# One layer of a hybrid encoder in float32: a bank, early loads and a summed mean in the projection, and w2's first groups stored in the first block

## Chip, cores, metric

One core of a Trainium2 chip runs the whole program. The metric is the device time of one execution in microseconds (us); the median of several runs counts.

## The reference

One layer over 2048 tokens of width 1024. A normed input goes through one projection `w_in`; its columns feed three mixers, whose outputs go together through `w_out`; then follows an MLP with squared ReLU, and a last norm. Cut to what matters:

```python
h = _rmsnorm(x, g_attn)
p = h @ w_in                                        # 2816 columns
y_a = a_b * _causal_dwconv(a_c * a_h, w_conv_a)     # mixer A, width 3, 256 channels
g = b_glu[..., :256] * sigmoid(b_glu[..., 256:])
g = _causal_dwconv(g, w_conv_b) + b_conv_b          # mixer B, width 31
y_b = silu(_layernorm(g, ln_b_g, ln_b_b))           # mean and variance over 256 channels
# mixer C: stick-breaking attention, 8 heads of 64, strictly causal
z = q @ k.T / 8; log_beta = log_sigmoid(z); log_1m = where(mask, log_beta - z, 0)
a = where(mask, exp(log_beta + suffix_sums_of(log_1m)), 0); o = a @ v
x = x + concat([y_a, y_b, y_c]) @ w_out
h2 = _rmsnorm(x, g_ffn)
x = x + square(relu(h2 @ w_ff1)) @ w_ff2            # 1024 -> 4096 -> 1024
out = _rmsnorm(x, g_final)
```

## The kernel before

Everything lies with channels on the 128 partitions and tokens along the row. A token block `tb` is 512 tokens; there are four. Every large product is made of three matmuls (`mm3`): each factor is split into a rounded high half and the rest (`split`: a ScalarE copy makes the high half, a VectorE or GpSimd subtraction the low one).

*Projection.* It runs in two halves of two token blocks (`p_start`, `p_half`). Each unit of 256 columns of `w_in` is split in the first half, stored in DRAM (`WS`) and loaded in the second. Around it `weave` runs side generators, each advanced in proportion to the main loop's progress (cost, first and last point): `mixer_b`, in the second half also `attention` for the first queries of each head (i = 0), and `pre_split`, which splits `w_out` and the first four chunks of `w1` and stores them. Mixer B has its 31 taps on VectorE in the one PSUM bank "c"; then a mean over 256 channels by matmul with a constant matrix, the variance, a power on GpSimd (`rsqrt`, L118) and its spread over partitions by matmul (`spread`, L134). PSUM banks here: d 3, c 1, z 2, q 1, o 1.

*Attention.* `a_pass1` makes the scores of a key group (bank z), their sigmoids and running products, and ends with `a_cross_a`, the chain across partitions on VectorE: a transpose into a PSUM tile `X`, a scan and some small products into `T`. `a_pass2` multiplies by the transposed chain (`Q`, bank q), splits and multiplies with the values (bank o). Pass 2 of one head runs beside pass 1 of the next.

*Blocks.* `block(tb)` then does, for each token block, the product with `w_out`, the MLP in 32 chunks of `w1` (`ffn1`) and 8 groups of four chunks with `w2` (`ffn2`), and the end (`finish_`); attention for later queries is woven in. `unit` and `w2_piece` bring the weights in by `piece`: in the first block(s) raw weights are loaded and split, then the halves are stored, and later blocks load the halves. Four buffers hold pieces of `w1`/`w_out`, three those of `w2`, five raw loads and other tiles of tag `xt`. `need1` and `need2` ask for the next ones. In the first block the second half of a `w2` piece gets its low half by an accumulating transfer issued by GpSimd (`split_dma`).

Almost all transfers go through the SP queue, in one order; a transfer that has to wait holds all behind it. The order of instructions on each engine and queue is set before the run by a planner, from the program's order, priorities and its own estimates of durations.

Of the kernel before, what the change touches and what calls it, by code (L numbers as in the profile page):

```python
# [15 lines left out]
P = 128  # L16
# [5 lines left out]
HD = 64  # L22
# [46 lines left out]
class Trunk:  # L69
# [78 lines left out]
    def consts(self, ctx):  # L148
# [5 lines left out]
        t = c.tile([P, DC], F32, name="g_attn")  # L154
        nc.scalar.dma_start(t, a["g_attn"].rearrange("(d p) -> p d", p=P))
        self.gvec["g_attn"] = t
# [23 lines left out]
    def vectors(self):  # L180
        nc, tc, a, c = self.nc, self.tc, self.a, self.c
        for name in ("g_ffn", "g_final"):
            t = c.tile([P, DC], F32, name=name)
            self.dma(t, a[name].rearrange("(d p) -> p d", p=P))
            self.gvec[name] = t
        self.wa = c.tile([P, 2, 3], F32, name="wa")
        self.dma(self.wa, a["w_conv_a"].rearrange("(c p) k -> p c k", p=P))
        self.wb = c.tile([P, 2, 31], F32, name="wb")
        self.dma(self.wb, a["w_conv_b"].rearrange("(c p) k -> p c k", p=P))
        self.vb = {}  # L190
        for name in ("b_conv_b", "ln_b_g", "ln_b_b"):
            t = c.tile([P, 2], F32, name=name)
            self.dma(t, a[name].rearrange("(c p) -> p c", p=P))
            self.vb[name] = t
# [246 lines left out]
    def mixer_b(self, hf):  # L441
        nc = self.nc
        for tb in (2 * hf, 2 * hf + 1):
            acc = []
            for c in range(2):
# [10 lines left out]
                nc.scalar.activation(acc[c], t, AF.Copy)  # L456
            for _ in range(3):
                yield 1.8
            mean = self.psum("ps_mean", "c")
            for c in range(2):  # L460
                nc.tensor.matmul(mean, self.avg, acc[c], start=c == 0, stop=c == 1)
            sqs = []
# [9 lines left out]
            yv = self.rsqrt(self.colsum(sqs[:1], "c"), 1.0 / 256.0, LN_EPS)  # L472
            for _ in range(4):
                yield 1.8
# [71 lines left out]
    def a_pass1(self, g):  # L546
# [36 lines left out]
        A0.append(t)  # L583
        yield 1
        tot = self.a_cross_a(g, Rd, None)
        if not i:
# [23 lines left out]
    def a_cross_a(self, g, R, seed):  # L610


        nc = self.nc
        X = self.ps.tile([P, TB], F32, name="ps_t", tag="z", bufs=self.banks["z"])
        T = self.at.tile([P, TB + 1], F32, name="T", tag="T1" if seed is None else "T2", bufs=1)
        nc.vector.transpose(X, R)
# [18 lines left out]
        nc.vector.tensor_tensor(q3, q3, C.unsqueeze(2).to_broadcast([P, 16, 32]), op=ALU.mult)  # L635
        g["qd" if seed is None else "ql"] = qt
        return tot

    def a_pass2(self, g):
# [37 lines left out]
        for x in late:  # L677
            self.a_av(g, o, n, *x)
        tmp = pool.tile([P, TB], F32, name="otmp", tag="om", bufs=ab["om"])[:HD]
        nc.scalar.activation(tmp, o[HD:P], AF.Copy)  # L680

        if h % 2 == 0:
            self.yc = self.st.tile([P, TB], F32, name="yc", tag="y", bufs=self.ab["yc"])
        nc.vector.tensor_tensor(self.yc[HD * (h % 2) : HD * (h % 2) + HD], o[0:HD], tmp, op=ALU.add)
        if h == H - 1 and i:
# [26 lines left out]
    def attention(self, groups):  # L712
# [3 lines left out]
        for n in range(len(groups) + 1):  # L716
# [5 lines left out]
            d1 = d2 = 0.0  # L722
            live1, live2 = g is not None, prev is not None

            lag = 0 if prev and prev["i"] else 2
            while live1 or live2:
                if live2 and (not live1 or (d2 + lag) * max(n1, 1) <= d1 * max(n2, 1)):
                    try:
# [5 lines left out]
                elif live1:  # L734
                    try:
                        next(p1)
                        d1 += 1
# [90 lines left out]
    def block(self, tb, before):  # L828
# [140 lines left out]
        yield from ffn1(0, 1)  # L969
        need2(1)  # L970

# [4 lines left out]
        yield from ffn1(2)  # L976
        need2(2)
        ms = self.spread(mt, "z")
        for d in range(DC):
            if d == DC // 2:  # L980
                yield from ffn1(3)
            nc.vector.tensor_tensor(acc[d], acc[d], ms, op=ALU.mult)
        ss2 = hp.tile([P, TB], F32, name="ss2", tag="ss", bufs=2)
        sq7 = []
        for c in range(4, FC):
            yield from ffn1(c)
            if c < w2b:
                need2(c)
            if c % G == 0 and not (tb == 3 and c == FC - G):
# [8 lines left out]
        else:  # L998
# [8 lines left out]
            self.finish(tb, acc, [ss2] + sq7, em, right)  # L1007
            for _ in fin:
# [6 lines left out]

    def finish_(self, tb, acc, sums, em, cols=slice(0, TB)):
        nc, a, hp = self.nc, self.a, self.hp
# [4 lines left out]
        yield  # L1022
        R = self.spread(y, "z", bs)
        yield
        for d in range(DC):
            t = acc[d] if tb == 3 else hp.tile([P, TB], F32, name="ot", tag="ot", bufs=self.ob)
            t = t[:, cols]
            nc.vector.scalar_tensor_tensor(t, acc[d][:, cols], self.gvec["g_final"][:, d : d + 1], R[:, cols], op0=ALU.mult, op1=ALU.mult)
            (nc.scalar if tb == 3 and d % 2 else nc.sync).dma_start(a["out"][d * P : (d + 1) * P, ts], t)
            yield  # L1030

    def build(self):
        tc = self.tc
        with ExitStack() as ctx:
# [6 lines left out]
            with ExitStack() as c1:  # L1041
# [12 lines left out]
                self.ab = dict(Kl=1, A0=6, om=2, Alo=2, Ahi=2, Vl=1, late=1, yc=2)  # L1054
                weave(self.p_half(0), [(Side(self.mixer_b(0)), 115, 20, 225, True), (Side(self.x_norms()), 24, 60, 180, True)])
                self.heads = {}
                a0 = Side(self.attention([(h, 0) for h in range(H)]))
                weave(self.p_half(1), [(Side(self.mixer_b(1)), 116, 0, 200, True), (a0, 28, 0, 210, True), (Side(self.pre_split()), len(self.presplit), 0, 200, True)])
            with ExitStack() as c2:
# [67 lines left out]
```

## Time and profile before

| | us |
|---|---|
| three runs | 2421.49, 2425.93, 2416.74 |
| their median | 2421.49 |
| the profiled execution | 2415.74 |
| its span, first to last instruction | 2414.0 |
| TensorE busy in it | 2379.1 |
| VectorE, GpSimd, ScalarE busy | 1534.0, 1128.6, 1043.6 |

The granted clock of TensorE was 0.997 on average. Times in the profile count from the start of the span: the projection lies up to about 545, block 0 to about 1035, blocks 1 and 2 take about 485 us each, and block 3 the rest. A busy TensorE is not one at its peak, since matmuls are pipelined; the count of matmuls in a stretch tells more.

### The profile page before, as it was taken

To read this page: it belongs to the slowest core of one execution; us is meant where nothing else is said; L and a number is where in the kernel's file an instruction comes from. 1 tells how busy PE (TensorE), PEld (TensorE's weight loads), DVE (VectorE), ACT (ScalarE), POOL (GpSimd) and SP (SyncE) were. 2 spreads that over 40 slices of the span, in tenths; PEclk is the share of its full clock that TensorE was granted. 3 is DMA by queue.
4 is the path that set the end of the run, shared out by engine and by line. 5 is a ranking of instruction groups with operands and counts; after the bars stand their busy time and mean duration, and the time that the engine had idled before them with its cause. 6 is when DMAs were issued, how large, how long until landed. Compare 5 with 4: busy or idle time off the path is not lost.

```text
span 2414.0 us, 32476 instructions
## 1 busy us (share of the span) xinstructions
PE 2379.1 (99%) x11316; PEld 2005.3 (83%) x11316; DVE 1534.0 (64%) x2436; ACT 1043.6 (43%) x1906; POOL 1128.6 (47%) x1133
## 2 busy tenths in 40 slices
PE   8999999999999999999999999999999999999998
PEld 7888877898888888878888888888888888888887
DVE  7966698943898887766676768476667625212114
ACT  5232423342666666544555555355555522121121
POOL 0342477640676666425666665268788720000000
PEclk9999999999999999999999999999999999999999
DMA  7569987789788778687777777866677556655555
GB/s 258 200 234 341 299 269 233 223 265 280 209 225 245 229 206 222 186 300 245 253 234 229 220 242 214 289 200 198 187 202 204 175 183 221 224 187 192 201 183 192
DMA packets 237059, 549.04 MB, mean 227 GB/s; under 512 B 26720, under 2 KB 100448, under 8 KB 218464
## 3 DMA queue, kind: packets, MB, share of 16 engines
q1 hardware_dynamic: 180304, 480.89, 58.9%
q0 software_dynamic: 37504, 56.64, 11.0%
q10 hardware_dynamic: 19088, 9.44, 1.4%
q8 instruction: 89, 1.46, 0.2%
q14 instruction: 74, 0.61, 0.1%
HBM read 390.38 MB, written 148.11 MB: 223 GB/s over the span
## 4 chain that ended last, share of the span: by engine, by line
PE 84%; DMA 6%; DVE 6%; issue 1%; ACT 1%; POOL 1%; SPq 1%; POOLq 0%; DVEq 0%; ACTq 0%
PE ps_y L107 9%; PE ps_y L105 9%; PE ps_y L103 9%; PE ps_u L103 9%; PE ps_u L105 9%; PE ps_u L107 9%; PE ps_p L107 4%; PE ps_p L105 4%; PE ps_p L103 3%; PE ps_z L522 2%; PE ps_z L523 2%; PE ps_x L103 2%; PE ps_x L105 2%; PE ps_x L107 2%; PE ps_o L710 2%; PE ps_o L709 2%
## 5 line engine op out<-in xcount | busy, mean ns | idle before, releaser
L90 POOL TENSOR_TENSOR Alo<-A,Ahi 128x512 fp32r<-128x512 f32 x288 | 385.3, 1347 | 147.0 <-ACT Ahi L88 69.9
L958 DVE TENSOR_TENSOR acc<-acc,ps_y 128x512 f32<-128x512 f32 (+1 forms) x264 | 175.7, 667 | 193.5 <-PE ps_y L107 191.4
L103 PE MATMUL ps_u<-hh,w 128*128 128x512 f32 x1024 | 279.4, 392 | 6.4 <-DMA w<-s_w 6.1
L103 PE MATMUL ps_y<-fh,w 128*128 128x512 f32 (+1 forms) x1056 | 281.2, 384 | 0.0
L105 PE MATMUL ps_y<-fh,w 128*128 128x512 f32 (+1 forms) x1056 | 279.7, 383 | 0.1
L602 POOL TENSOR_TENSOR A<-A,R 128x512 f32<-128x512 f32 x168 | 222.4, 1326 | 121.7 <-ACT A L600 103.3
L107 PE MATMUL ps_y<-fl,w 128*128 128x512 f32 (+1 forms) x1056 | 278.6, 383 | 0.1
L105 PE MATMUL ps_u<-hh,w 128*128 128x512 f32 x1024 | 276.1, 390 | 0.3 <-DVE w L90 0.3
L107 PE MATMUL ps_u<-hl,w 128*128 128x512 f32 x1024 | 275.8, 390 | 0.0
L118 POOL TENSOR_TENSOR rs_y<-rs_v,mhalf 128x4 f32<-128x4 f32 (+1 forms) x13 | 13.2, 1017 | 530.9 <-DVE rs_v L117 486.0
L922 ACT ACTIVATE ps_u<-ps_u 128x512 f32<-128x512 f32 x128 | 74.7, 583 | 399.3 <-PE ps_u L107 399.1
L932 DVE TENSOR_TENSOR fl<-ps_u,fh 128x512 fp32r<-128x512 f32 x128 | 87.7, 685 | 223.3 <-ACT fh L931 222.9
L105 PEld LDWEIGHTS ps_y<-fh,w 128*128 128x128 f32 x1056 | 195.0, 188 | 39.8 <-DMA w<-wraw 0.5
L107 PEld LDWEIGHTS ps_y<-fl,w 128*128 128x128 f32 x1056 | 195.0, 188 | 39.4 <-DVE fl L932 0.6
L88 ACT ACTIVATE Ahi<-A 128x512 fp32r<-128x512 f32 x288 | 176.6, 627 | 117.8 <-PE ps_o L709 51.3
L105 PEld LDWEIGHTS ps_u<-hh,w 128*128 128x128 f32 x1024 | 192.1, 188 | 41.5 <-DVE w L90 0.7
L107 PEld LDWEIGHTS ps_u<-hl,w 128*128 128x128 f32 x1024 | 192.1, 188 | 40.1
L103 PEld LDWEIGHTS ps_y<-fh,w 128*128 128x128 f32 x1056 | 193.6, 188 | 36.8
L103 PEld LDWEIGHTS ps_u<-hh,w 128*128 128x128 f32 x1024 | 186.9, 188 | 42.4 <-DMA w<-s_w 8.1
L604 DVE TENSOR_TENSOR R<-ps_z,R 128x512 f32<-128x512 f32 x168 | 115.7, 689 | 150.6 <-ACT ps_z L601 128.3
L452 DVE SCALAR_TENSOR_TENSOR ps_c<-g,wb,ps_c 128x512 f32<-128x512 f32 x240 | 179.9, 749 | 4.9
L90 DVE TENSOR_TENSOR w<-wraw,w 128x512 fp32r<-128x512 f32 x152 | 150.4, 1008 | 23.7 <-ACT w L88 23.2
(171 smaller groups left out, 4750.7 us busy)
## 6 DMA issues: line engine op xcount, KB each, us to landing
w<-s_w SPq DMA_DIRECT2D x200, 512.0 KB, 3.9
w<-s_w SPq DMA_DIRECT2D x68, 1024.0 KB, 4.8
wraw<-in_w SPq DMA_DIRECT2D x192, 256.0 KB, 5.0
w<-s_w_out SPq DMA_DIRECT2D x64, 512.0 KB, 5.0
s_w<-w SPq DMA_DIRECT2D x32, 1024.0 KB, 5.5
s_w<-w SPq DMA_DIRECT2D x56, 512.0 KB, 4.5
Qd<-KQ SPq DMA_DIRECT2D x64, 256.0 KB, 6.3
xraw<-in_xT SPq DMA_DIRECT2D x48, 256.0 KB, 4.5
```

The costliest lines, as they stand in the source:

```text
L88: nc.scalar.activation(hi, x, AF.Copy)
L90: e.tensor_tensor(lo, x, f(hi), op=ALU.subtract)
L103: self.nc.tensor.matmul(ps, wh, xh, start=start and k == 0, stop=False)
L105: self.nc.tensor.matmul(ps, wl, xh, start=False, stop=False)
L107: self.nc.tensor.matmul(ps, wh, xl, start=False, stop=stop and k == n - 1)
L452: nc.vector.scalar_tensor_tensor(t, g[:, k : k + TB], self.wb[:, c, k : k + 1], t, op0=ALU.mult, op1=ALU.add)
L522: nc.tensor.matmul(z[:, oc], keys, g["qh"][:, qc], start=k == 0, stop=False)
L602: nc.gpsimd.tensor_tensor(t, t, R, op=ALU.mult)
L604: nc.vector.tensor_tensor(Rn, z, R, op=ALU.mult)
L922: nc.scalar.activation(ps, ps, AF.Relu)
L932: nc.vector.tensor_tensor(lo, ps, f(hi), op=ALU.subtract)
L958: nc.vector.tensor_tensor(acc[d][:, cols], acc[d][:, cols], ps, op=ALU.add)
```

## The change

- `consts`, `vectors`: the small parameter vectors are laid out on the host as their tiles lie in SBUF, so each partition's numbers are contiguous in DRAM.
- `mixer_b`: the two channel halves are added on GpSimd (`both`), and one matmul instead of two makes the mean; four instead of three steps stand before it, and six instead of four before the spread. The weave's costs and ends go with it: `mixer_b` 130 to 225 in the first half and 130 to 224 in the second (before 115 and 116 to 225 and 200), attention to 212, `pre_split` to 205.
- `attention`, `a_pass1`, `a_cross_a`: for i = 0 the chain's `X` takes bank q instead of one of z, and pass 1 waits, in the program's order, until the previous head's pass 2 is through.
- `a_pass2`: the upper half of the head's output is copied into the result's place and the lower added there, without the tile `otmp`.
- `pre_split`: the raw load of the next piece is asked for before the present one is split.
- `piece`: `w2`'s groups 0 and 1 (eight pieces) are split and stored in block 0 and loaded from block 1 on; groups 2 to 7 stay as they were (split in blocks 0 and 1, stored in block 1). Accumulating transfers are used for groups 2 to 7 alone.
- `block`: from block 1 on, `w2`'s first pieces are asked for later and one at a time.
- the last block's end: the right half's first two rows of tiles are scaled by `g_final` on ScalarE beforehand and multiplied on GpSimd by a copy of the norm, the other six on VectorE as before.

```diff
@@ mixer_b
-            for _ in range(3):
+            both = self.mx.tile([P, TB], F32, name="sum", tag="sq", bufs=2)
+            nc.gpsimd.tensor_tensor(both, acc[0], acc[1], op=ALU.add)
+            for _ in range(4):
                 yield 1.8
             mean = self.psum("ps_mean", "c")
-            for c in range(2):
-                nc.tensor.matmul(mean, self.avg, acc[c], start=c == 0, stop=c == 1)
+            nc.tensor.matmul(mean, self.avg, both, start=True, stop=True)
...
-            for _ in range(4):
+            for _ in range(6):
                 yield 1.8
             R = self.spread(yv, "c")
@@ a_pass1, a_cross_a
+        if not i:
+            while not g["free"]():
+                yield None
         tot = self.a_cross_a(g, Rd, None)
...
-        X = self.ps.tile([P, TB], F32, name="ps_t", tag="z", bufs=self.banks["z"])
+        X = self.psum("ps_t", "z" if g["i"] else "q")
@@ attention
+            if g:
+                g["free"] = lambda: not live2
...
-                if live2 and (not live1 or (d2 + lag) * max(n1, 1) <= d1 * max(n2, 1)):
+                if live2 and (not live1 or d1 > n1 or (d2 + lag) * max(n1, 1) <= d1 * max(n2, 1)):
...
-                        next(p1)
+                        if next(p1) is None:
+                            d1 = n1 + 1e-3
+                            continue
@@ piece
-        first = -1 if (name, *at) in self.presplit else {"w_out": 0, "w1": 0, "w2": 1}[name]
+        first = -1 if (name, *at) in self.presplit else int(name == "w2" and at[0] > 1)
...
-                if name == "w2" and tb == 0 and part is parts[-1][0]:
+                if name == "w2" and tb < first and part is parts[-1][0]:
@@ pre_split
-        for name, c, q in self.presplit:
-            raw = self.w_raw(self.unit_source(name, c, q))
+        nxt = self.w_raw(self.unit_source(*self.presplit[0]))
+        yield 1
+        for n, (name, c, q) in enumerate(self.presplit):
+            raw = nxt
+            if n + 1 < len(self.presplit):
+                nxt = self.w_raw(self.unit_source(*self.presplit[n + 1]))
@@ block
         yield from ffn1(0, 1)
-        need2(1)
+        if not tb:
+            need2(1)
...
         yield from ffn1(2)
-        need2(2)
+        need2(2 if not tb else 0)
...
                 yield from ffn1(3)
+                need2(1)
...
-            if c < w2b:
-                need2(c)
+            if c == G:
+                need2(w2b - 1)
@@ finish_ (right half of the last block)
+            Rs = hp.tile([P, TB], F32, name="Rs", tag="ot", bufs=self.ob)
+            nc.scalar.activation(Rs[:, cols], R[:, cols], AF.Copy)
...
+            if d in scaled:
+                nc.gpsimd.tensor_tensor(t, t, Rs[:, cols], op=ALU.mult)
```

More of the change, by code (lines that the diff above doesn't have):

```diff
@@ L154, in consts @@
         t = c.tile([P, DC], F32, name="g_attn")
-        nc.scalar.dma_start(t, a["g_attn"].rearrange("(d p) -> p d", p=P))
+        nc.scalar.dma_start(t, a["g_attn"])
         self.gvec["g_attn"] = t
@@ L183, in vectors @@
             t = c.tile([P, DC], F32, name=name)
-            self.dma(t, a[name].rearrange("(d p) -> p d", p=P))
+            self.dma(t, a[name])
             self.gvec[name] = t
         self.wa = c.tile([P, 2, 3], F32, name="wa")
-        self.dma(self.wa, a["w_conv_a"].rearrange("(c p) k -> p c k", p=P))
+        self.dma(self.wa, a["w_conv_a"])
         self.wb = c.tile([P, 2, 31], F32, name="wb")
-        self.dma(self.wb, a["w_conv_b"].rearrange("(c p) k -> p c k", p=P))
+        self.dma(self.wb, a["w_conv_b"])
         self.vb = {}
@@ L192, in vectors @@
             t = c.tile([P, 2], F32, name=name)
-            self.dma(t, a[name].rearrange("(c p) -> p c", p=P))
+            self.dma(t, a[name])
             self.vb[name] = t
@@ L678, in a_pass2 @@
             self.a_av(g, o, n, *x)
-        tmp = pool.tile([P, TB], F32, name="otmp", tag="om", bufs=ab["om"])[:HD]
-        nc.scalar.activation(tmp, o[HD:P], AF.Copy)
         if h % 2 == 0:
             self.yc = self.st.tile([P, TB], F32, name="yc", tag="y", bufs=self.ab["yc"])
-        nc.vector.tensor_tensor(self.yc[HD * (h % 2) : HD * (h % 2) + HD], o[0:HD], tmp, op=ALU.add)
+        y = self.yc[HD * (h % 2) : HD * (h % 2) + HD]
+        nc.scalar.activation(y, o[HD:P], AF.Copy)
+        nc.vector.tensor_tensor(y, y, o[0:HD], op=ALU.add)
         if h == H - 1 and i:
@@ L1006, in block @@
                         next(fin, None)
-            self.finish(tb, acc, [ss2] + sq7, em, right)
+            scaled = (0, 1)
+            for d in scaled:
+                nc.scalar.activation(acc[d][:, right], acc[d][:, right], AF.Copy, scale=self.gvec["g_final"][:, d : d + 1])
+            self.finish(tb, acc, [ss2] + sq7, em, right, scaled)
             for _ in fin:
@@ L1014, in finish, with finish_ @@
                 pass
-    def finish_(self, tb, acc, sums, em, cols=slice(0, TB)):
+    def finish_(self, tb, acc, sums, em, cols=slice(0, TB), scaled=()):
         nc, a, hp = self.nc, self.a, self.hp
@@ L1023, in finish_ @@
         R = self.spread(y, "z", bs)
+        if scaled:
+            Rs = hp.tile([P, TB], F32, name="Rs", tag="ot", bufs=self.ob)
+            nc.scalar.activation(Rs[:, cols], R[:, cols], AF.Copy)
         yield
@@ L1027, in finish_ @@
             t = t[:, cols]
-            nc.vector.scalar_tensor_tensor(t, acc[d][:, cols], self.gvec["g_final"][:, d : d + 1], R[:, cols], op0=ALU.mult, op1=ALU.mult)
+            if d in scaled:
+                nc.gpsimd.tensor_tensor(t, t, Rs[:, cols], op=ALU.mult)
+            else:
+                nc.vector.scalar_tensor_tensor(t, acc[d][:, cols], self.gvec["g_final"][:, d : d + 1], R[:, cols], op0=ALU.mult, op1=ALU.mult)
             (nc.scalar if tb == 3 and d % 2 else nc.sync).dma_start(a["out"][d * P : (d + 1) * P, ts], t)
@@ L1054, in build @@
                 self.ab = dict(Kl=1, A0=6, om=2, Alo=2, Ahi=2, Vl=1, late=1, yc=2)
-                weave(self.p_half(0), [(Side(self.mixer_b(0)), 115, 20, 225, True), (Side(self.x_norms()), 24, 60, 180, True)])
+                weave(self.p_half(0), [(Side(self.mixer_b(0)), 130, 20, 225, True), (Side(self.x_norms()), 24, 60, 180, True)])
                 self.heads = {}
                 a0 = Side(self.attention([(h, 0) for h in range(H)]))
-                weave(self.p_half(1), [(Side(self.mixer_b(1)), 116, 0, 200, True), (a0, 28, 0, 210, True), (Side(self.pre_split()), len(self.presplit), 0, 200, True)])
+                weave(self.p_half(1), [(Side(self.mixer_b(1)), 130, 0, 224, True), (a0, 28, 0, 212, True), (Side(self.pre_split()), len(self.presplit) + 1, 0, 205, True)])
             with ExitStack() as c2:
@@ L1108 @@
         ),
-        "g_attn": lay(np.asarray(inputs["g_attn"])[0]),
-        "w_conv_a": lay(np.asarray(inputs["w_conv_a"])[0].T),
-        "w_conv_b": lay(np.asarray(inputs["w_conv_b"])[0].T),
-        "b_conv_b": lay(np.asarray(inputs["b_conv_b"])[0]),
-        "ln_b_g": lay(np.asarray(inputs["ln_b_g"])[0]),
-        "ln_b_b": lay(np.asarray(inputs["ln_b_b"])[0]),
-        "g_ffn": lay(np.asarray(inputs["g_ffn"])[0]),
-        "g_final": lay(np.asarray(inputs["g_final"])),
+        "g_attn": lay(np.asarray(inputs["g_attn"])[0].reshape(DC, P).T),
+        "w_conv_a": lay(np.asarray(inputs["w_conv_a"])[0].reshape(3, 2, P).transpose(2, 1, 0)),
+        "w_conv_b": lay(np.asarray(inputs["w_conv_b"])[0].reshape(31, 2, P).transpose(2, 1, 0)),
+        "b_conv_b": lay(np.asarray(inputs["b_conv_b"])[0].reshape(2, P).T),
+        "ln_b_g": lay(np.asarray(inputs["ln_b_g"])[0].reshape(2, P).T),
+        "ln_b_b": lay(np.asarray(inputs["ln_b_b"])[0].reshape(2, P).T),
+        "g_ffn": lay(np.asarray(inputs["g_ffn"])[0].reshape(DC, P).T),
+        "g_final": lay(np.asarray(inputs["g_final"]).reshape(DC, P).T),
     }
```

## The prediction

> **What bounds the kernel now.** I read the page's busy shares first, then the busy times of a few stretches, then what TensorE waited for in those that lose time, and last the rows around the longest waits.
>
> ```profile
> PE 2379.1 (99%) x11316; PEld 2005.3 (83%) x11316; DVE 1534.0 (64%) x2436; ACT 1043.6 (43%) x1906; POOL 1128.6 (47%) x1133
> ```
>
> TensorE is busy in 2379.1 of 2414.0 us. So a change pays here only if it takes matmuls out or fills some of the 34.9 us in which TensorE stands. Busy times by stretch (us busy of TensorE, weight loads, VectorE, ScalarE and GpSimd, granted clock, DMA share, GB/s) tell where those are:
>
> ```profile
> 300.00:420.00 120.00, 110.14 (x506) 89.62 (x505) 112.02 (x158) 38.06 (x74) 92.12 (x95) 0.97 0.78 256
> 420.00:480.00 60.00, 60.00 (x287) 50.37 (x287) 58.57 (x95) 17.97 (x31) 38.94 (x43) 1.00 0.67 211
> 620.00:740.00 120.00, 118.03 (x555) 97.94 (x555) 107.95 (x171) 76.06 (x143) 85.04 (x87) 1.00 0.76 215
> 1020.00:1140.00 120.00, 114.90 (x526) 95.22 (x525) 75.91 (x122) 50.79 (x92) 42.21 (x43) 1.00 0.77 262
> 2040.00:2100.00 60.00, 58.37 (x264) 48.11 (x263) 20.14 (x32) 12.36 (x21) 0.00 (x0) 1.00 0.67 242
> 2100.00:2160.00 60.00, 60.00 (x267) 49.67 (x266) 10.44 (x16) 10.58 (x18) 0.00 (x0) 1.00 0.56 199
> ```
>
> The last row is the undisturbed rate: 267 matmuls in 60 us, 0.225 us each. The first (projection, second half of the tokens) loses 9.9 us while VectorE is busy in 112.0 of 120; the third (block 0) 2.0; the fourth (start of block 1) 5.1; the fifth (start of block 3) 1.6. TensorE's waits in 240 to 420, at the start of block 1 and at the start of block 3 (total, times, longest):
>
> ```profile
> PE ps_z L522 <- DVE T L635: 3.4, 1, 3.4
> PE ps_z L522 <- ACT A L537: 2.7, 1, 2.7
> PE ps_R L134 <- POOL rs_y L118: 1.7, 1, 1.7
> PE ps_p L103 <- DVE u L355: 1.0, 1, 1.0
> ```
> ```profile
> PE ps_u L103 <- DMA w<-s_w: 4.7, 4, 1.6
> ```
> ```profile
> PE ps_u L103 <- DMA w<-s_w: 1.4, 2, 1.0
> ```
>
> **The change part by part.**
>
> *Mean of a sum.* The chain of waits and the group table give the mean's price, and GpSimd's full-width product that of the new addition:
>
> ```profile
> 226.77 1.72 PE ps_mean L461 x4
> ```
> ```profile
> L461 PE MATMUL ps_mean<-cb,avg 128*128 128x512 f32 x16 | 7.7, 604 | 0.4 <-ACT cb L456 0.4
> ```
> ```profile
> L602 POOL TENSOR_TENSOR A<-A,R 128x512 f32<-128x512 f32 x168 | 222.4, 1326 | 121.7 <-ACT A L600 103.3
> ```
>
> Four token blocks take 4 passes each, 1.72 us. One matmul instead of two halves that: 4 x 0.86 = 3.4 us less on the bounding engine. The sum costs GpSimd 4 x 1.33 us, and GpSimd has 28 us free in 300 to 420. In front of it stand selects and low halves of the same queue; behind it only the mean waits. The one further step (1.8 x 224/130 = 3.1 us of the main loop) covers the 1.33. Ends: -3.4, and +1.9 if each mean waits out its addition (4 x 1.33 - 3.4). I take -3.4, since idle GpSimd time is near.
>
> *The chain's bank.* For the first queries of each head the cross chain sits in one of two score banks from the transpose to the last product:
>
> ```profile
> 317.79 0.72 DVE L616 STREAM_TRANSPOSE ps_t<-R 128x512 f32<-128x512 f32 x1
> ...
> 324.69 0.68 DVE L635 TENSOR_TENSOR T<-T,ps_t 128x512 f32<-128x512 f32 x1
> ```
>
> That holds it for 7.6 us, because convolution taps are queued between the chain's steps, and the next head's scores pay the 3.4 us wait. In bank q only VectorE writes and reads, so no other engine waits for it. The new condition puts the chain behind the previous head's second pass, whose last use of q is a VectorE product: queued behind it are taps and evacuations of the same engine, which TensorE needs. Two more steps (6.2 us) before the spread cover the 1.7 us wait for rs_y. So 5.1 us are addressed. What is late next is VectorE itself: 112.0 us of its work in 300 to 420 cannot end before 412, so no more than 8.0 of the 9.9 can come back, and the evacuation wait (1.0, u) grows. I give 1.1 back and take -4.0. Ends: -8.0 and 0.
>
> *Loads ahead.* The 2.7 us wait for ScalarE starts elsewhere: ScalarE stood before a split, and the SP queue before a store of ya (waits of SP in 240 to 480).
>
> ```profile
> 364.05 1.15 ACT L88 ACTIVATE wph<-wraw 128x512 fp32r<-128x512 f32 x2 [6.52 <-issue]
> ```
> ```profile
> SPq L79 <- DVE ya L365: 21.2, 3, 11.5
> ```
>
> The idle 6.52 us names no raw load; the split's two output buffers have to be stored first, and those stores queue behind ya. A raw load issued one step earlier does not free them. I count 0; the 2.7 stays in the range.
>
> *w2's first two groups, block 0.* Eight pieces: each loses ScalarE's negated copy and GpSimd's accumulating transfer and gains a VectorE subtraction and a 1 MB store. Rows: the subtraction's group and one with nothing beside it, the SP queue's waits in 620 to 740, the transfers' sizes and landings.
>
> ```profile
> L90 DVE TENSOR_TENSOR w<-wraw,w 128x512 fp32r<-128x512 f32 x152 | 150.4, 1008 | 23.7 <-ACT w L88 23.2
> ```
> ```profile
> 654.60 0.68 DVE L90 TENSOR_TENSOR w<-wraw,w 128x512 fp32r<-128x512 f32 x1
> ```
> ```profile
> SPq L79 <- DVE w L90: 39.7, 15, 6.0
> ```
> ```profile
> w<-s_w SPq DMA_DIRECT2D x68, 1024.0 KB, 4.8
> ...
> s_w<-w SPq DMA_DIRECT2D x32, 1024.0 KB, 5.5
> ```
>
> VectorE: 8 x 1.008 = 8.1 us (5.4 at the lone 0.68) against 12.0 free: fits, barely. DMA: 8 MB over 120 us is 70 GB/s on 215, and 0.76 x 285/215 = 1.01 of the engines: full. SP: each store waits for its split, 39.7/15 = 2.65 us, and w1's raw loads are queued behind it; w1's four buffers (two chunks ahead) are the cover. If that cover goes, the start of block 1 shows the price: 5.1. Ends: -2.0 (all idle time of the stretch goes with the accumulating transfers) and +5.1. I take +1.5, nearer to the row that shows this stretch itself.
>
> The Trainium skill, "DMA: Bandwidth & Descriptors", section "Where 436 GB/s comes from", puts the HBM limit of one core near 358 GB/s, by which 285 GB/s leaves a fifth free and this term would be about 0 (estimate: sum -13.5 instead of -12.0). The stretch's own 0.76 at 215 GB/s speaks for the lower ceiling, and the sum goes by it.
>
> *Block 1 and blocks 2 and 3.* In block 1 the same pieces no longer need 16 raw loads, 16 splits and 8 stores but 8 loads of 1 MB, landing in 4.8. The SP queue, its waits in 1020 to 1160 and its issues:
>
> ```profile
> SPq L79 <- DVE w L90: 24.1, 10, 6.7
> ```
> ```profile
> 1078.72 0.33 SPq L79 DMA_DIRECT2D s_w<-w  x1
> 1081.71 0.33 SPq L79 DMA_DIRECT2D wraw<-in_w  x1
> 1082.69 16.35 SPq L79 DMA_DIRECT2D w<-s_w  x6
> ```
>
> The w1 loads of 1082.69, for which TensorE waits, stood behind a w2 store and a raw load. Both go, and the pieces are asked for later and one by one: the first after the third chunk, the third one before ffn2, each with at least a chunk (24 x 0.225 = 5.4 us) for its 4.8. Of the 4.7 I take -4.0 (ends -5.1 and 0; Qd's loads and the stores of the finish stay in the queue). Block 3 asks for 1 MB pieces between its w1 loads; of 1.4 I take -1.0 (ends -1.6 and +1.0, a piece now late).
>
> *Vectors and tail.* The first split of x waits for g_attn; the same kind of small load lands sooner where it has 1 KB; at the end VectorE does eight products.
>
> ```profile
> 4.92 0.72 ACT L223 ACTIVATE xh<-xraw,g_attn 128x512 fp32r<-128x512 f32 x1 [0.43 <-DMA g_attn<-in_g_attn]
> ```
> ```profile
> g_attn<-in_g_attn ACTq DMA_DIRECT2D x1, 4.0 KB, 4.1
> ...
> b_conv_b<-in_b_conv_b SPq DMA_DIRECT2D x1, 1.0 KB, 2.1
> ```
> ```profile
> 2407.77 3.22 DVE L1028 SCALAR_TENSOR_TENSOR acc<-acc,g_final,ps_R 128x256 f32<-128x256 f32 x8 [2.09 <-PE ps_R L134]
> 2408.67 2.69 ACTq L1029 DMA_DIRECT2D outT<-acc  x4
> ```
> ```profile
> 401.54 0.79 POOL L564 TENSOR_TENSOR A<-A,om 128x256 f32<-128x256 f32 x1
> ```
>
> Head: -0.4, the wait itself (ends 0 and -2.0, the difference of the landings). The other vectors' loads lie beside a busy TensorE: 0. Tail: six products instead of eight save 2 x 0.40; GpSimd needs 2 x 0.79 plus ScalarE's copy of R (0.4, taken as one VectorE product), 2.0 in all, under VectorE's 2.4. -0.7 (ends -0.8 and +0.4, GpSimd's stores holding up the others). The head's join without the tile otmp moves the same two instructions: 0.
>
> *Sum.* -3.4 - 4.0 + 0 + 1.5 - 4.0 - 1.0 - 0.4 - 0.7 = -12.0 us. The profiled execution took 2415.74 (span 2414.0), so 2403.7 on its terms; it lies 5.8 under the median shown, 2421.49, and below all three runs. For the median I predict 2409.5.
>
> **The rivals.** *VectorE keeps the projection's waits* (only where they fall changes): -8.0, 2413.5. For it: 112.0 of 120 busy. Against: 420 to 480, where VectorE is busy in 58.57 of 60 and TensorE loses nothing. *All addressed waits go*: projection -8.0, block 0 at 0, block 1 -5.1, block 3 -1.4, head -0.4, tail -0.8, mean -3.4: -19.1, 2402. For it: the waits are few and long, with named causes. *The stall moves into block 0*, the other side: eight stores, each holding the SP queue for 2.65 us, 21.2 in all, and once w1's lead is used up TensorE waits all of it; with the other terms (-13.5) that is +7.7, 2429. It decides from 13.5 us, 1.7 a piece. Against: the same stretch already has 15 such waits, 39.7 us, and TensorE idles 2.0. *It doesn't do what it says*: a planner orders each queue by its own estimates, so a load written earlier need not be issued earlier; then mean, head and tail are left, -4.5, 2417.
>
> **How the numbers follow.** Forecast 0.40 (its own range 2405 to 2413), all waits 0.21, VectorE 0.24, nothing moves 0.07, block 0 0.08. The range 2399 to 2421 takes in all but the last and the far ends. A measurement here can tell about 0.5%, 12.1 us. Faster: the 0.21, half of the forecast, 0.05 of the VectorE case: 0.46. Slower: most of the block 0 case, 0.06. Same: 0.48.
>
> **What would show it.** Mean: 8 records instead of 16, at 0.43 us apart. Chain: no wait of ps_z for T before 420; TensorE's idle time in 300 to 420 near 6 instead of 9.9 us. Block 1: no wait for w<-s_w in its first 40 us. Block 0: idle in 620 to 740 at 2 to 5 us; above 13 the prediction is wrong. Wrong too if VectorE evacuations (u, sig, ac) appear among TensorE's waits with over 5 us, or if means wait for the GpSimd sum.

## Result and profile after

The changed kernel took 2434.48 us (median of 6 runs, 2427.22 to 2438.13), the kernel before 2421.58 beside it (6 runs, 2415.49 to 2425.93): ratio 1.0051, 95% interval 1.0035 to 1.0068. It is slower by 0.5%, some 13 us, where 12 us less were forecast; the time lies above the whole range. The profiled execution of after took 2434.2 us (span 2432.1).

The busy shares of after, and the same stretches as before, with the one from 540 to 600 added; for that one the row of before stands in the second fence (columns as before):

```profile
PE 2382.1 (98%) x11308; PEld 2010.1 (83%) x11308; DVE 1537.5 (63%) x2426; ACT 1033.1 (42%) x1885; POOL 1127.8 (46%) x1131
```
```profile
300.00:420.00 120.00, 103.47 (x463) 84.37 (x462) 110.71 (x147) 36.90 (x72) 92.14 (x93) 0.93 0.77 246
420.00:480.00 60.00, 60.00 (x288) 50.40 (x287) 58.63 (x95) 17.52 (x30) 39.25 (x44) 1.00 0.69 217
540.00:600.00 60.00, 53.84 (x302) 47.36 (x301) 28.60 (x46) 21.18 (x39) 20.17 (x25) 0.94 0.84 251
620.00:740.00 120.00, 118.36 (x556) 98.44 (x556) 100.64 (x157) 69.54 (x128) 66.48 (x73) 1.00 0.85 269
1020.00:1140.00 120.00, 114.91 (x524) 95.67 (x523) 74.81 (x115) 44.28 (x79) 37.12 (x39) 0.99 0.71 231
2040.00:2100.00 60.00, 58.64 (x265) 48.32 (x264) 25.80 (x41) 17.06 (x29) 0.00 (x0) 1.00 0.80 281
```
```profile
540.00:600.00 60.00, 60.00 (x320) 51.98 (x319) 20.68 (x32) 16.60 (x29) 5.83 (x9) 1.00 0.91 283
```

Two stretches lost: in 300 to 420 TensorE stands 16.5 us instead of 9.9, and in 540 to 600, the seam between projection and block 0, 6.2 instead of 0. The granted clock fell there too, to 0.93 and 0.94. Blocks 0 and 1 in their middle and the start of block 3 are as they were.

TensorE's waits of after, 240 to 420, then 540 to 600, then the start of block 1 (total, times, longest), and the group of the mean:

```profile
PE ps_ss L127 <- POOL sq L470: 5.3, 1, 5.3
PE ps_o L706 <- ACT Ahi L88: 4.5, 1, 4.5
PE ps_o L706 <- DVE yc L689: 2.1, 1, 2.1
PE ps_p L103 <- DVE u L355: 1.7, 1, 1.7
PE ps_o L706 <- POOL Alo L90: 1.5, 3, 0.7
PE ps_mean L462 <- POOL sum L458: 1.5, 1, 1.5
```
```profile
PE ps_x L103 <- DMA w<-s_w_out: 4.5, 1, 4.5
PE ps_v L397 <- DVE vt L405: 1.7, 1, 1.7
```
```profile
PE ps_u L103 <- DMA w<-s_w: 3.9, 1, 3.9
PE ps_x L103 <- DMA w<-s_w_out: 1.1, 1, 1.1
```
```profile
L462 PE MATMUL ps_mean<-sum,avg 128*128 128x512 f32 x8 | 4.2, 605 | 1.5 <-POOL sum L458 1.5
```

The waits for T and A of before are gone, and others stand in their place. Below, *TensorE's loss* is worked out from all matmul records: the distance from one matmul's start to the next less the median distance of its kind, summed over a stage. It holds idle time and slowed matmuls alike, and it is that of one profiled execution of each kernel. In the projection (to the last unit, about 505 us) it is 18.6 us before and 27.6 after; in the seam and block 0 6.4 and 16.3; block 1 10.8 and 10.8; block 2 4.4 and 7.4; block 3 4.8 and 4.2.

### The profile page after: what moved, and what is told of

Its sections match the earlier page's. It is cut to its first block, busy times and chain, and to the rows that moved or that the text cites. A ratio compares the mean times of both kernels' runs of the same rounds, so it can differ in the third digit from the quotient of the medians.

```text
span 2432.1 us, 32383 instructions
## 1 busy us (share of the span) xinstructions
PE 2382.1 (98%) x11308; PEld 2010.1 (83%) x11308; DVE 1537.5 (63%) x2426; ACT 1033.1 (42%) x1885; POOL 1127.8 (46%) x1131
## 4 chain that ended last, share of the span: by engine, by line
PE 85%; DMA 8%; DVE 4%; issue 1%; POOL 1%; ACT 1%; SPq 0%; ACTq 0%; DVEq 0%; POOLq 0%
PE ps_y L107 9%; PE ps_y L103 9%; PE ps_y L105 9%; PE ps_u L103 9%; PE ps_u L105 9%; PE ps_u L107 9%; PE ps_p L103 4%; PE ps_p L107 4%; PE ps_p L105 4%; PE ps_z L523 2%; PE ps_z L524 2%; DMA w<-s_w 2%; PE ps_o L715 2%; PE ps_o L714 2%; PE ps_x L103 2%; PE ps_x L105 2%
## 5 line engine op out<-in xcount | busy, mean ns | idle before, releaser
L90 DVE TENSOR_TENSOR w<-wraw,w 128x512 fp32r<-128x512 f32 x144 | 142.3, 1007 | 28.0 <-ACT w L88 27.6
```

The costliest lines, as they stand in the source:

```text
L90: e.tensor_tensor(lo, x, f(hi), op=ALU.subtract)
```

## Experiments

An *end* is the point of the main loop (230 in all) by which a side generator is to be through; its *pace* follows from that and from the cost that `weave` is given for it. Theory A1: mixer B's second half, ending at 224 instead of 200, holds the start of block 0. Theory G: GpSimd's work stretches VectorE's in the projection. The rivals put the loss on w2, on the chain's bank or on the mean, or on nothing but a new order, which may come out better or worse whatever the edit. Ratios are to the kernel before on the same chip; "early" is mixer B's second end back at 200.

| kernel | us (runs) | ratio, 95% interval | loss in projection |
|---|---|---|---|
| e1 w2 alone | 2421.12 (10) | 1.0009, 0.9996 to 1.0022 | 19.0 |
| e2 all but w2 | 2430.23 (4) | 1.0044, 1.0028 to 1.0059 | 26.5 |
| e3 late mixer alone | 2425.52 (10) | 1.0026, 1.0013 to 1.0039 | 17.5 |
| e5 after, early | 2424.71 (10) | 1.0023, 1.0011 to 1.0034 | 25.3 |
| e6 bank alone | 2419.89 (10) | 0.9992, 0.9977 to 1.0006 | 17.7 |
| e7 mean alone | 2417.44 (10) | 0.9974, 0.9962 to 0.9986 | 19.0 |
| e8 early, no bank | 2425.98 (10) | 1.0016, 1.0006 to 1.0027 | 28.2 |
| e9 early, no mean | 2418.88 (10) | 0.9988, 0.9975 to 1.0 | 18.0 |
| e10 low halves on VectorE | 2421.17 (10) | 0.9998, 0.9984 to 1.0012 | 17.9 |
| e11 mean and loads | 2419.76 (10) | 0.9991, 0.9978 to 1.0003 | 20.8 |
| e12 early, more steps | 2424.77 (10) | 1.0016, 1.0005 to 1.0028 | 25.5 |
| e13 mean, vectors, more steps | 2416.77 (10) | 0.9983, 0.997 to 0.9995 | 18.5 |
| e14 early, no loads | 2426.51 (9) | 1.0029, 1.0018 to 1.0041 | 27.1 |
| e15 early, old head join | 2422.19 (10) | 0.9998, 0.9982 to 1.0015 | 20.9 |
| e16 after, old ends and paces | 2417.97 (10) | 0.9988, 0.9976 to 1.0001 | 11.7 |
| e17 early, sum only | 2421.01 (10) | 0.9996, 0.9986 to 1.0006 | 23.1 |
| e18 old ends, no w2, no tail | 2414.2 (5) | 0.9962, 0.9949 to 0.9975 | 17.6 |
| e19 old ends, late mixer | 2421.39 (10) | 0.9998, 0.9986 to 1.0009 | 15.3 |

**The late end of mixer B: e3, e5.** The last store of sq and ScalarE's first split for block 0, from the timelines of GpSimd and ScalarE in after; then the last store in before:

```profile
543.57 1.13 POOL L485 DMA_DIRECT2D Y<-sq  x2
```
```profile
552.75 2.72 ACT L88 ACTIVATE y<-yraw 128x512 fp32r<-128x512 f32 x5 [5.59 <-DMA Y<-sq]
```
```profile
517.43 1.15 POOL L484 DMA_DIRECT2D Y<-sq  x2
```

Block 0's tiles lie where mixer B's were, so its first splits wait for that store; behind them on ScalarE stand the evacuations of the last units (ps_v waits 1.7), and w_out's loads go out late. Two kernels test it, one from each side. e3, in before:

```diff
-(Side(self.mixer_b(1)), 116, 0, 200, True)
+(Side(self.mixer_b(1)), 116, 0, 224, True)
```

> The kernel before with one number changed: mixer B of the second half is spread to 224 of the main loop's 230 instead of 200. Theory A1 (the late end of mixer B is what holds block 0: the first splits of block 0 take over SBUF of mixer B's tiles, so ScalarE waits for the last store of mixer B, with evacuations of V behind it): idle time of 5 to 9 us appears in 540 to 600, 2427 to 2431; ScalarE waits for Y from sq there. Rival A2 (the late end is harmless, since the planner takes the taps as soon as VectorE is free): 2418 to 2425, no idle time there.

e5, in after:

```diff
-(Side(self.mixer_b(1)), 130, 0, 224, True)
+(Side(self.mixer_b(1)), 130, 0, 200, True)
```

> The changed kernel with mixer B of the second half ending at 200 again instead of 224 (cost 130 kept). Theory A1: the 9 us around the start of block 0 go, 2423 to 2427. Rival A2: they stay, 2432 or more. If VectorE's work in the projection is the limit, the taps now lie 12% denser and idle time in 300 to 420 grows by up to 8 us.

The stretch 540 to 600 of e3, then of e5:

```profile
540.00:600.00 60.00, 54.74 (x285) 46.52 (x285) 29.75 (x47) 21.78 (x39) 21.62 (x26) 0.94 0.88 266
```
```profile
540.00:600.00 60.00, 60.00 (x329) 52.43 (x329) 20.65 (x33) 15.66 (x27) 4.01 (x7) 1.00 0.84 261
```

The one line makes the stall in before (5.3 us idle, clock 0.94) and takes it out of after. A1 is shown: 0.26% in before (less than was expected), 0.28% in after (1.0051 less 1.0023). But e5 is still slower than before, with 25.3 us lost in the projection.

**Single parts: e1, e2, e6, e7.** e1 has the hunks of `piece` and of `need2` alone, e2 all others:

```diff
-        first = -1 if (name, *at) in self.presplit else {"w_out": 0, "w1": 0, "w2": 1}[name]
+        first = -1 if (name, *at) in self.presplit else int(name == "w2" and at[0] > 1)
...
-            if c < w2b:
-                need2(c)
+            if c == G:
+                need2(w2b - 1)
```

> Only w2's part: groups 0 and 1 split and stored in block 0, pieces asked for singly from block 1. After minus before is +13 us (2434.5 against 2421.6); TensorE's idle time grew by 9 us in the second half of the projection and by 8 us around the start of block 0, both ahead of w2's first piece. Theory A (the projection's part costs, w2's part does not): 2413 to 2424, the idle times before 600 us as before. Rival B (w2's part moved its stall into block 0 and block 2): 2430 or more, with waits for w in block 0. Rival C (any edit makes the planner order everything anew, and the time moves by 5 to 15 us either way with it): idle time changes in stretches that the edit doesn't touch, the projection among them.

> The changed kernel with w2's part undone. Theory A: 2433 to 2442, with the idle time of the projection and of the start of block 0 (TensorE waiting for w_out) as in the changed kernel. Rival B: 2410 to 2422. Rival C: neither 2421 plus this part nor 2434 minus the other: the two halves of the change do not add up to +13.

w2's part is worth nothing that shows (1.0009), and after without it is as slow (1.0044). In e1 block 0 lost 10.2 instead of 6.4 us, block 1 10.7 instead of 10.8. (The 10.2 says little of w2: in e6 and e10, which leave it alone, TensorE also has a wait for w in block 0, of 3.0 and 3.5 us; in e1 the longest is 3.4.) Why block 1 gained nothing stands in SP's waits of after, 1020 to 1160, its timeline, and TensorE's:

```profile
SPq L79 <- PE ps_u L107: 18.5, 7, 4.6
...
SPq L79 <- DVE w L90: 6.8, 1, 6.8
```
```profile
1091.58 0.80 SPq L79 DMA_DIRECT2D w<-s_w  x2
```
```profile
1090.47 1.30 PE L107 MATMUL ps_u<-hl,w 128*128 128x512 f32 x5
...
1097.38 1.73 PE L103 MATMUL ps_u<-hh,w 128*128 128x512 f32 x4 [3.89 <-DMA w<-s_w]
```

The load is issued when the chunk before it gives its buffer back (the last matmul of 1090.47), and TensorE, with some 2 us of other work, stands until 5.8 us after it. The queue's waits for VectorE's splits, which the prediction blamed, fell from 24.1 us to 6.8 (in e1 to none), and the stall stayed.

e6 has the bank and its condition alone:

```diff
-        X = self.ps.tile([P, TB], F32, name="ps_t", tag="z", bufs=self.banks["z"])
+        X = self.psum("ps_t", "z" if g["i"] else "q")
```

> The kernel before with the chain's bank and its condition alone. By the prediction's step: the wait of ps_z for T (3.4 us) goes, about 4 us gained, ratio 0.998. By the theory that VectorE, busy in 112 of 120 us there, only moves its waits: the wait for T goes and one of ps_o or of an evacuation takes its place; TensorE's loss in the projection stays at 18 to 20 us against 18.6, and the ratio lies between 0.999 and 1.003.

Its waits of TensorE, 240 to 420:

```profile
PE ps_o L705 <- ACT Ahi L88: 4.5, 2, 2.8
PE ps_mean L461 <- ACT cb L456: 3.7, 1, 3.7
```

The wait for T went and two others of the same length took its place: 17.7 us lost against 18.6. This is the rival of the kept waits.

e7 has the summed mean and its further steps alone, with costs that keep the old pace and ends (the numbers of `weave` abridged, here and below):

```diff
-            for c in range(2):
-                nc.tensor.matmul(mean, self.avg, acc[c], start=c == 0, stop=c == 1)
+            nc.tensor.matmul(mean, self.avg, both, start=True, stop=True)
...
-mixer_b(0) 115, 20, 225    mixer_b(1) 116, 0, 200
+mixer_b(0) 126, 20, 225    mixer_b(1) 127, 0, 200
```

> The kernel before with the summed mean and its further steps alone; the weave's costs follow the added steps (126 and 127), the ends stay at 225 and 200. With the mixer's end back at 200 the changed kernel still lost 25 us of TensorE's time in the first part of the projection (before 19), its longest wait there 5.3 us of ps_ss for GpSimd's sum of squares. Theory M (GpSimd's queue now stands twice in the norm's chain, and the matmuls behind it pay): the wait of ps_ss for GpSimd appears here, 2419 to 2425. Rival Q (the norm's chain is not at fault, it is the bank and the order behind it): 3.4 us of matmuls less and the rs_y wait gone, 2412 to 2417.

It gains 0.26%, 6.3 us (interval 3.4 to 9.2), though its mean waits: ps_ss for GpSimd 3.5 us, ps_mean for the sum 1.4.

**Contention: e10.** In before, `pre_split`'s low halves go from GpSimd to VectorE:

```diff
-            self.split(hi, lo, raw, "pool")
+            self.split(hi, lo, raw)
```

> The kernel before with one word changed: pre_split's low halves are subtracted on VectorE instead of GpSimd. In the trace VectorE's products of two SBUF tiles, 0.41 us alone, took up to 4.2 us (5.2 in the changed kernel) exactly while GpSimd ran back to back; between 265 and 420 VectorE was so stretched by 30 us before and 34 after. Theory G (GpSimd's runs hold VectorE up, and this is what makes the projection's waits): 24 x 1.3 us less on GpSimd and 24 x 0.7 us more on VectorE; the stretched products get shorter, the loss in the projection falls below 15 us, 2410 to 2416. Rival V (VectorE is simply full, 112 of 120 us busy): 17 us more work on VectorE lengthen the waits, 2424 or more.

Summed over `R<-om,R` from 265 to 420 us, 12.3 us above the shortest duration shrank to 4.1, so GpSimd's work does stretch it. The loss in the projection hardly moved (17.9), but the edit also gives VectorE 24 more subtractions, some 17 us, so neither expectation came, and the run parts the two in their sum alone, and in the kernel before alone. In after the same sum is 16.9, in e16 (below) 6.0. Whether that makes the loss of after or goes along with it, no run shows; G stays open there.

**The mean and its company: e8, e9, e11 to e17.** Early and without the bank (e8), and early without the mean, its steps and costs (e9):

```diff
-        X = self.psum("ps_t", "z" if g["i"] else "q")
+        X = self.ps.tile([P, TB], F32, name="ps_t", tag="z", bufs=self.banks["z"])
```

> The changed kernel with mixer B ending at 200 (2424.7 measured) and, besides, the chain back in bank z with its condition gone. Theory M: the loss in the projection stays near 25 us, 2422 to 2427. Rival Q (the condition puts the chain behind pass 2, values' matmuls then wait for Ahi and yc): the waits of ps_o for ACT Ahi and DVE yc (6.3 us there) go, the wait of ps_z for T (3.4 us) comes back, 2417 to 2421.

```diff
-            nc.tensor.matmul(mean, self.avg, both, start=True, stop=True)
+            for c in range(2):
+                nc.tensor.matmul(mean, self.avg, acc[c], start=c == 0, stop=c == 1)
```

> The changed kernel with mixer B ending at 200 and with the two matmuls of the mean and their fewer steps back. Theory M: the ps_ss wait of 5.3 us goes, 3.4 us of matmuls come back, and the power's wait of 1 to 3 us: 2421 to 2424, the loss in the projection near 20. Rival Q: loss near 25 and 3.4 us more matmuls, 2426 to 2430.

The bank is not it (28.2 without). The mean is in it: alone it gains 0.26%, beside the other parts it costs, with its steps and paces, 0.35% (e5 less e9). Rows of after show the path that it makes: VectorE, then GpSimd, then TensorE:

```profile
379.85 4.80 DVE L581 TENSOR_TENSOR R<-om,R 128x256 f32<-128x256 f32 x1 [1.33 <-POOL om L542]
384.68 2.80 DVE L583 TENSOR_TENSOR R<-om,R 128x256 f32<-128x256 f32 x1
387.52 0.73 DVE L621 STREAM_TRANSPOSE ps_t<-R 128x512 f32<-128x512 f32 x1
...
394.22 0.68 DVE L465 TENSOR_TENSOR cb<-cb,ps_mean 128x512 f32<-128x512 f32 x1
```
```profile
381.60 1.26 POOL L458 TENSOR_TENSOR sum<-cb,cb 128x512 f32<-128x512 f32 x1
...
398.31 1.71 POOL L470 TENSOR_TENSOR sq<-sq 128x512 f32<-128x512 f32 x1
```
```profile
382.92 1.12 PE L462 MATMUL ps_mean<-sum,avg 128*128 128x512 f32 x2 [1.45 <-POOL sum L458]
...
400.07 1.87 PE L127 MATMUL ps_ss<-ones,sq 128*128 128x2 f32 x8 [5.27 <-POOL sq L470]
```

ScalarE's copy of the finished convolution and, in before, the subtraction:

```profile
377.96 0.60 ACT L456 ACTIVATE cb<-ps_c 128x512 f32<-128x512 f32 x1 [4.20 <-DVE ps_c L452]
```
```profile
376.16 1.27 DVE L464 TENSOR_TENSOR cb<-cb,ps_mean 128x512 f32<-128x512 f32 x2
```

The copy ends at 378.6; the sum is done at 382.9, behind GpSimd's selects and splits. By then VectorE is in the whole cross chain of a head, and the mean's subtraction comes out of the queue at 394.22, 10 us after the mean. The squares follow, and TensorE stands 5.3 us before the variance. In before it ran ahead of the chain (381.23). Two products of VectorE stretched by GpSimd (379.85 and 384.68; see the last section) hold it until 387.5, 4.6 us of the time between the sum and the subtraction. But this path alone isn't the loss: in e7, which gained, the mean starts at 375.08, the subtraction comes at 387.07, and TensorE waits 3.5 us. e12 gives that path more program steps, in e5 (with costs of 141 instead of 130):

```diff
-            for _ in range(2):
+            for _ in range(5):
                 yield 1.8
             yv = self.rsqrt(self.colsum(sqs[:1], "c"), 1.0 / 256.0, LN_EPS)
```

> The change with mixer B's end back at 200 and three more steps (5.4 of cost) between the squares and the variance's matmul; costs 141 instead of 130 so that the pace of the steps stays. Theory of the missing cover: the sum on GpSimd makes the mean late, its subtraction falls behind the attention chain on VectorE, and nothing is left before the variance's matmul; with the steps the wait of ps_ss for GpSimd (5.3 us) goes, the loss in the projection falls from 25.3 to about 19, and the time from 2424.7 to about 2418. Rival, VectorE's and GpSimd's work is conserved and the wait only changes its name: the loss stays over 23, the time within 3 us of 2424.7.

e13 is the same edit in e7, with the vectors' host layout, and costs 137 and 138 instead of 126 and 127.

> The kernel before with the summed mean, the host layout of the small vectors and the same three more steps before the variance; mixer B ends at 225 and 200 as before. Without vectors and steps this took 2417.44, ratio 0.997. Theory of the missing cover: its 3.5 us wait of ps_ss goes and the head gains 0.6: about 2412 to 2414, ratio 0.995. Rival: another wait takes its place, ratio 0.997 to 0.998.

Both missed: the wait is 4.4 us in e12 (loss 25.5) and 3.5 in e13 (18.5). More steps in the program are no cover where a planner orders the queues afterwards (that this is why is argued, not shown). Next, which part the mean meets. e11 adds the loads to e7; e14 takes them from e5; e15 takes the head's join from e5; e17 keeps the sum but has the old steps and costs of mixer B, with attention's 212 and `pre_split`'s 205 left. The edits of e11, e14, e15 and e17 in this order:

```diff
+            if n + 1 < len(self.presplit):
+                nxt = self.w_raw(self.unit_source(*self.presplit[n + 1]))
...
-        nxt = self.w_raw(self.unit_source(*self.presplit[0]))
+            raw = self.w_raw(self.unit_source(name, c, q))
...
-        nc.scalar.activation(y, o[HD:P], AF.Copy)
+        tmp = pool.tile([P, TB], F32, name="otmp", tag="om", bufs=ab["om"])[:HD]
...
-range(4) ahead of mean, range(6) ahead of R, costs 130 and 130
+range(3) ahead of mean, range(4) ahead of R, costs 115 and 116
```

> The summed mean with the early raw loads of pre_split, mixer B ending at 200 as before. The mean alone took 2417.44 (19.0 us of TensorE lost in the projection). Theory that the early loads are what spoils the mean (ScalarE and GpSimd get the piece's split sooner, ahead of the sum and the square): over 23 us lost in the projection and about 2423. Theory that they do nothing, as predicted: 18 to 20 us lost, 2415 to 2420.

> The change with mixer B's end at 200 (2424.71 us; 25.3 us of TensorE lost in the projection) and without the early raw loads. If the loads are what the mean meets: 18 to 20 us lost, about 2417 us. If not: 24 to 27, 2422 to 2427. The mean with the early loads alone lost 20.8, which speaks for a small part at most.

> The change with mixer B's end at 200, and the head's join by its own tile otmp again. If the join is what the mean meets (the copy of the upper half into the result's place makes VectorE's sum the last reader of bank o, and ps_o waits 4.0 us for yc): the wait for yc goes and 18 to 20 us are lost, about 2417. If not: 24 to 27, 2422 to 2427.

> The change with mixer B's end at 200 and the sum on GpSimd, but the steps and costs as before (3 ahead of the mean, 4 ahead of the spread, 115 and 116). Without the sum this took 2418.88 us and lost 18.0 us in the projection. If the sum itself is the cost (the mean is ready later, and its subtraction falls behind the attention chain on VectorE): 24 us or more lost, 2422 to 2427, and a wait of ps_ss for GpSimd over 3 us. If the steps are: 18 to 20 lost, and 3.4 us less of matmuls, about 2416.

The loads cost little beside the mean (0.9991 against e7's 0.9974, the difference about as large as its uncertainty) and taking them out helps nothing (1.0029). Without the join the wait for yc is gone and the loss is 20.9, with the old steps and costs 23.1. By time each of the two brings back most of what e9 does: 0.9998 and 0.9996, against e5's 1.0023 and e9's 0.9988. So no one part is at fault: the loss takes the sum, its steps and paces, and the join together. The sum itself, with the old steps, is left with 0.08% (e17 less e9), within the noise. e16 puts all ends and paces back:

```diff
-mixer_b(0) 130, 20, 225    mixer_b(1) 130, 0, 224    a0 28, 0, 212    pre_split + 1, 0, 205
+mixer_b(0) 126, 20, 225    mixer_b(1) 127, 0, 200    a0 28, 0, 210    pre_split + 1, 0, 200
```

> The change with all ends and the pace of the steps as before (mixer B 126 to 225 and 127 to 200, attention to 210, the early splits to 200). If the changed ends and paces are what the mean meets: 18 to 20 us lost in the projection, about 2417. If not: 24 to 27, 2422 to 2427.

Its stretch 300 to 420, TensorE's waits there (all of them), and its mean on VectorE and TensorE:

```profile
300.00:420.00 120.00, 116.37 (x549) 96.55 (x548) 115.08 (x169) 38.28 (x74) 94.27 (x97) 0.99 0.79 257
```
```profile
PE ps_o L706 <- POOL Alo L90: 2.5, 2, 1.9
PE ps_o L706 <- ACT Ahi L88: 0.8, 1, 0.8
```
```profile
372.24 0.69 DVE L640 TENSOR_TENSOR T<-T,ps_t 128x512 f32<-128x512 f32 x1
375.53 1.28 DVE L465 TENSOR_TENSOR cb<-cb,ps_mean 128x512 f32<-128x512 f32 x2
```
```profile
381.79 0.95 PE L127 MATMUL ps_ss<-ones,sq 128*128 128x2 f32 x8
```

With all parts in place and the old ends and paces, TensorE loses 11.7 us in the projection of this execution, the least of all kernels here. The sum is done at 368.3, the subtraction follows 7 us later (here too behind a chain, but a shorter one), and nothing waits for the variance. The time is 2417.97, 0.35% under e5. (The profiled execution took 2411.4, the lowest of its ten, so the rows show it at its best.) e19 lets mixer B alone end late in e16:

```diff
-(Side(self.mixer_b(1)), 127, 0, 200, True)
+(Side(self.mixer_b(1)), 127, 0, 224, True)
```

> The change with attention to 210, the early splits to 200 and mixer B at 127 in 200 put to 127 in 224: only mixer B's second half ends late. If the late end costs by itself, as in the kernel before (3 to 4 us) and in the change (10 us): 2422 to 2428 and TensorE idle for 5 to 6 us at 540 to 600, where block 0 waits for the last store of sq. If it costs only beside the changed paces: within 2 us of 2418.

The seam stalls again: 5.6 us idle, ps_x 4.0 behind vt. The four corners, as ratios:

| | paces and other ends old | as changed |
|---|---|---|
| mixer B to 200 | 0.9988 (e16) | 1.0023 (e5) |
| mixer B to 224 | 0.9998 (e19) | 1.0051 (after) |

The changed paces cost 0.35 and 0.53% beside the other parts (each difference uncertain by about 0.2), 8 to 13 us; on the kernel before, alone, they weren't run. The late end costs 0.10 and 0.28, 2 to 7 us; in before, 0.26. Whether the two add up or help each other, the intervals don't tell. Which of the paces matters wasn't parted further than by e17. That a new order costs by itself is not borne out: e6 and e10 have a new order in the projection too and stay within 0.1% of before. Two kernels are few, though, and why this order is a bad one is argued from its waits, not shown.

**A version that beats both: e18.** All parts of the projection with e16's ends, w2 and the tail as before. Against e16:

```diff
-        first = -1 if (name, *at) in self.presplit else int(name == "w2" and at[0] > 1)
+        first = -1 if (name, *at) in self.presplit else {"w_out": 0, "w1": 0, "w2": 1}[name]
...
-            self.finish(tb, acc, [ss2] + sq7, em, right, scaled)
+            self.finish(tb, acc, [ss2] + sq7, em, right)
```

> The kernel before with vectors, summed mean, chain's bank, head's join and early loads, all ends and paces as before; no change to w2 and the tail. With those two it took 2417.97 us (ratio 0.9988), and its tail 7.3 us from the last matmul to the end against 6.2. If the tail's products on GpSimd cost 1 us and w2's split 2 to 4 us in block 0: 2413 to 2416, ratio 0.9955 to 0.9975, the projection's loss staying at 12 to 15. If the projection's order hangs on single estimates rather than on the parts: loss back at 18 or more, ratio over 0.998.

2414.2 us, ratio 0.9962 (0.9949 to 0.9975): 9 us under the kernel before, some 20 under the changed one. Against e16 the w2 and tail parts cost 0.26% (uncertain by 0.2). The projection's loss is 17.6, not the 12 to 15 expected, though up to the projection's end e18 has the order of e16 on VectorE, GpSimd and ScalarE, but for two neighbours changed about on VectorE. Where the 6 us come from, one product shows, in e16 and then in e18:

```profile
335.43 1.39 DVE L583 TENSOR_TENSOR R<-om,R 128x256 f32<-128x256 f32 x1
```
```profile
336.48 6.27 DVE L583 TENSOR_TENSOR R<-om,R 128x256 f32<-128x256 f32 x1
```

In e18 GpSimd runs from 336.18 to 342.47 without a pause, and the product ends at 342.75. VectorE was 1.0 us behind e16 when it began and is 5.9 us behind after it. So a stretched product can reach TensorE, and the losses of two executions of nearly one order can lie 6 us apart: smaller differences in the table's last column need not be effects of an edit.

## Why the prediction was wrong

*The step that failed: the ends and paces were never priced.* The prediction costed each edit by the instructions it adds and removes. "130 to 224", "to 212" and "to 205" stand in its front matter as something that goes with the mean; no term has them. They change the order on all engines from some 140 us on, and the 13 us hang on them: with them undone the same parts take 0.9988, and without w2 and tail 0.9962. The terms of the parts left there (mean, bank, loads, head: -7.8 us) make 0.9968, but the sum comes near by luck, since the mean gave more than its term and the bank less. The late end's share, 0.28% at most, is shown with its cause, the store that block 0 waits for. The paces' share, 0.35 to 0.53%, is shown as a cost beside the other parts; how they make it stays open.

*Mean, -3.4.* Right in its records: 8 instead of 16, 4.2 us instead of 7.7. The -6.3 measured alone holds some 3 us more that no row explains. "Behind it only the mean waits" was wrong: behind it stand the subtraction, queued on VectorE with the attention chain, the squares and the variance (5.3 us). "The one further step covers the 1.33" was wrong too: the mean waits 1.5 us for the sum, one of the prediction's own signs of being wrong, and e12's further steps left the wait behind it at 4.4.

*Chain's bank, -4.0.* The size failed: e6 gives 0.9992, with no change inside the interval. The waits changed their names, which is the rival that had 0.24.

*Loads, 0.* Right as far as the noise tells: nothing gained, and little lost.

*w2, +1.5 - 4.0 - 1.0 = -3.5.* e1 shows +0.9 per thousand (-1.0 to +5.3 us). Block 0's middle lost nothing: 1.6 us idle in 620 to 740. Its DMA share was 0.85 at 269 GB/s, by which the engines would be full at 316 and not at the 285 that the term went by, so a share can't be scaled to a ceiling like this. A stretch of before shows more:

```profile
180.00:240.00 60.00, 60.00 (x363) 53.23 (x361) 39.60 (x59) 15.61 (x28) 14.43 (x12) 1.00 1.02 348
```

348 GB/s, at a share of 1.02, agrees with the limit near 358 of the Trainium skill, "DMA: Bandwidth & Descriptors", section "Where 436 GB/s comes from", which the prediction put aside. Block 1's -4.0 failed: the prediction took the row before TensorE's wait (a store and a raw load ahead in the queue) for its cause; the buffers' return sets the issue. Idle time of the stretch: 5.1 before, 5.1 after.

*Head, -0.4.* First matmul at 5.55 instead of 6.21 us: -0.7, inside its ends. *Tail, -0.7.* The sign failed. From the last matmul to the end 7.27 us instead of 6.22; rows of ScalarE, VectorE and ScalarE's queue in after:

```profile
2424.87 0.38 ACT L1047 ACTIVATE Rs<-ps_R 128x256 f32<-128x256 f32 x1 [2.85 <-PE ps_R L134]
2425.29 2.44 DVE L1055 SCALAR_TENSOR_TENSOR acc<-acc,g_final,ps_R 128x256 f32<-128x256 f32 x6 [2.00 <-ACT Rs L1047]
...
2426.19 1.95 ACTq L1056 DMA_DIRECT2D outT<-acc  x4
```

VectorE's first product waits for ScalarE's copy. VectorE ends 2.9 instead of 3.3 us after the last matmul, but the end is 4.4 instead of 3.0 us behind that; what of the stores sets it no row shows. Without the part (e18) it is 6.3.

*Prices by idle time.* A stall was priced at its idle length. In after, 300 to 420 idles 16.5 us, but the loss there is 25.0: the clock of 0.93 takes most of the rest (0.07 x 103.5 = 7.2). Right behind the stall of 5.27 us the eight small matmuls took 1.87 us (400.07), without one 0.95 (381.79 in e16). The Trainium skill, "TensorE: Matmul & The Clock Gate", section "Part 1: The HAM clock gate", says that the array's default is the throttled state and that recent activity releases it. By that a stall costs more than itself, and the trace agrees.

## What to carry over

An end or a pace of a side generator is an edit like any other: ask what is laid over its tiles next, and which queue meets which when the order shifts. Before work is moved to an engine with free time, follow its result to the next queue on which it must stand: here a sum of 1.3 us is followed by 10 us behind a chain on another engine. In e6, where no work went, a wait that was removed came back under another name. So try the parts one by one, and the parts together without the new schedule, and go by the times of many executions: a trace is one of them.

## Hardware, not expected

VectorE's products of two SBUF tiles stretch while GpSimd runs back to back. One line of before, its duration in ns (least, median, most), and the longest of them beside GpSimd's row behind which it ends:

```profile
L580 DVE TENSOR_TENSOR R<-om,R x32: 406/620/4208, 284.8 to 1876.9; 128x256 f32<-128x256 f32 x32
```
```profile
311.28 4.21 DVE L580 TENSOR_TENSOR R<-om,R 128x256 f32<-128x256 f32 x1
```
```profile
313.92 1.29 POOL L337 TENSOR_TENSOR sig<-sig,R 128x512 f32<-128x512 f32 x1
```

0.41 us became 4.21: GpSimd's run ended at 315.21 and the product at 315.49. GpSimd's next instruction, at 315.64, needs this product, so the pause is itself a wait for it. In after one reached 5.22 us, in e18 6.27. The Trainium skill, "GPSIMD Engine Reference", section "1. Specifications", names this contention for VectorE instructions with two SBUF inputs; the trace agrees and gives the size, ten to fifteen times the duration. So a VectorE busy in 112 of 120 us was partly a VectorE that waited, which the bound of 8.0 us in the prediction didn't see.
